# A hybrid encoder layer on one core: the seven-product sums accumulated in PSUM, and w_out's operands split in their own stage

## The chip, the cores and the metric

The kernel runs on one core of one Trainium2 chip. The metric is the device time of one launch in microseconds (us), the median of the runs shown. A core has TensorE (PE, matmuls into PSUM), VectorE (DVE), ScalarE (ACT), GpSimd (POOL) and SyncE (SP, whose queue issues the DMAs here). PSUM has eight banks of 128 x 512 float32; a matmul writes one of them.

## The reference

One layer on x of 1024 tokens by 1024 features, all float32:

```
h = rmsnorm(x); q, k, v, r, decay, u, g_a, g_b = split(h @ w_in)
o = gated linear attention, 4 heads, forward and backward scans in chunks
y_a = (rmsnorm(o) * gain * silu(r)) @ w_branch
y_b = (centred means of u over 2/4/8/16 tokens, minus u, @ w_pool) * scale
x = x + (sigmoid(g_a) * y_a + sigmoid(g_b) * y_b) @ w_out
gate, up = split(rmsnorm(x) @ w_ffn_in)          # 2 x 2816 columns
x = x + (silu(gate) * up) @ w_ffn_out
return rmsnorm(x)
```

## The kernel before

Every float32 operand is split into two float32r parts, hi (a cast on ACT, L181) and lo (a subtraction, L182, on DVE or POOL), and each product is three matmuls, hi x hi, hi x lo, lo x hi (`products`, L252). Five large projections go further: each 2 x 2 block product is done with seven block products in place of eight (Winograd's form of Strassen's scheme). Call them P1 to P7; the four results are P1+P2, P1+P6+P5+P3, P1+P6+P7+P4 and P1+P6+P7+P5, so that partial sums such as P1+P6 are shared. Before, each of the seven products is accumulated in a PSUM bank of its own and evicted into partial sums in SBUF by ACT (a copy of P1) and DVE (adds).

The stages, with their start in the profiled execution: attention (about 80 to 345 us, overlapped with the projection of r), gate units (419), branch projection (633), merged projection through w_out (720), FFN in (804), FFN out (1236 to 1456).

- **Attention.** Each head's products wait for decay scans on DVE, exponentials on ACT and the split of keys (`kt`). Beside it run jobs from a generator, `beside` (L556): one job per tick, ticks counted by matmuls in `pump`. A job may be a sum on POOL (L584), then a cast on ACT (L578), a subtraction on DVE (L569), and some ticks later a put to DRAM (L565). `branch_jobs` prepares w_branch's sums; `output_jobs` (L500) prepares all seven operands of w_out, split into hi and lo, `wo_out`.
- **Gate units** (`Gates`, L1136, ten units of seven products of 12 matmuls, 512 wide). Each unit's weights are combined on DVE (L848), cast on ACT and subtracted on POOL, four products ahead. Units 0 and 1 feed the pooling branch, whose work on DVE (L946 to L960) runs beside units 2 and on. Banks come in turn from all eight.
- **Branch and merged projections** (`project`, L1230). Seven products, each of two pieces c = 0, 1, each piece four column blocks m of six matmuls, so that a product holds four banks. Branch pieces load w_branch's operands and split them; merged pieces (`merged_piece`, L1061) load hi and lo of `wo_out`. `collect_branch` evicts into u2 and v2 and merges with the gates; `merge` adds on DVE, multiplies on DVE, adds on POOL. `collect_out` (L1430) adds to x in SBUF, some of it on POOL.
- **FFN in** (`Gated`, L1483): 22 units of seven products. Partial sums p16 and p167 on DVE; `put_out` (L1534) makes four sums of each pair of units for the last projection and writes them to DRAM.
- **FFN out** (L1735 on): seven products of 11 steps of 128 rows, four banks each, results added to x in SBUF by `collect` (L1719), some on POOL. The g operand's lo part is made on POOL, the weight's on DVE.

The orders of the products are written out by hand: GATES, BRANCH, MERGED, ORDER and OUT_ORDER. Engines run their instructions in program order. PSUM banks come from two pools, ps_mm (3) and ps_g (5), and a tile's bank is free again after its last use.

## Time and profile before

| | us |
|---|---|
| median of 3 runs | 1461.8 (1461.52 to 1464.29) |
| profiled execution | 1464.93 |
| its span | 1463.1 |
| PE busy in it | 1391.6 |
| mean granted clock | 0.988 |

The profile comes from one execution. A row of a timeline gives start and length in us, engine, line, operation, the tile written and those read, and in brackets the idle time before it and who ended it. A row of a window gives busy time and count by engine, then the clock granted to PE (1.00 is full), the DMA share and GB/s. A group row ends with busy us, mean ns of one, and idle time before with its releasers. Matmuls overlap, so that their lengths (0.39 us) exceed the distance of their starts (0.22 us).

### The profile page before, as it was taken

The page shows a single profiled execution, that of the slowest core. Times are in us where ns is not written, and L with a number is a line of the kernel's source. Part 1 is how long each engine was busy: PE and PEld are TensorE (multiplying, and loading weights), DVE is VectorE, ACT ScalarE, POOL GpSimd, SP SyncE. Part 2 cuts the span into 40 slices and gives each one's busy share as a digit, 9 for nine tenths or more (in the row PEclk, how much of TensorE's full clock was granted, in tenths as well). Part 3 has the DMA queues.
Part 4 walks back from the last instruction along what each step waited for, and adds up shares of the span by engine and source line. Part 5 has one row for each costly group of instructions (what it writes and reads, how often), then busy time and mean ns, then how long its engine had stood idle before and what let it go on. Part 6 is the DMA issues. An engine that isn't in the chain of part 4 may idle for free. (4 is left out here: it accounts for less than half of the span.)

```text
span 1463.1 us, 18944 instructions
## 1 busy us (share of the span) xinstructions
PE 1391.6 (95%) x6677; PEld 1162.3 (79%) x6677; DVE 983.9 (67%) x1263; ACT 594.3 (41%) x1057; POOL 784.0 (54%) x552
## 2 busy tenths in 40 slices
PE   7999997979999899998999989999999999999998
PEld 6888796968888678777778768888888888778876
DVE  6176868686838855667985777777777777464375
ACT  6264665653323344443225532233233224443243
POOL 3272715232243356666644457666666678597345
PEclk9999999999999999999999999999999999999999
DMA  5233445461233365796567455454444446867352
GB/s 184 73 116 112 148 169 177 159 213 62 95 93 119 116 207 188 269 385 222 205 189 255 162 180 180 158 166 158 150 153 153 157 152 230 340 238 255 130 228 89
DMA packets 174464, 257.27 MB, mean 176 GB/s; under 512 B 11384, under 2 KB 98464, under 8 KB 174368
## 3 DMA queue, kind: packets, MB, share of 16 engines
q1 hardware_dynamic: 174368, 256.05, 51.6%
q8 instruction: 53, 0.87, 0.2%
q14 instruction: 43, 0.35, 0.1%
HBM read 169.76 MB, written 86.25 MB: 175 GB/s over the span
## 5 line engine op out<-in xcount | busy, mean ns | idle before, releaser
L182 POOL TENSOR_TENSOR wl<-fs,wh 128x512 fp32r<-128x512 f32 x120 | 164.4, 1372 | 178.9 <-ACT wh L181 140.0
L254 PE MATMUL ps<-gh,wl 128*128 128x512 f32 x616 | 240.6, 391 | 3.9 <-POOL wl L182 3.8
L254 PE MATMUL ps<-gh,wh 128*128 128x512 f32 x616 | 241.2, 392 | 0.5 <-DMA wh<-u_out 0.5
L254 PE MATMUL ps<-gl,wh 128*128 128x512 f32 x616 | 240.5, 390 | 0.8 <-POOL gl L182 0.8
L181 ACT CAST wh<-fs 128x512 fp32r<-128x512 f32 x120 | 74.2, 621 | 306.4 <-DVE fs L848 294.3
L182 POOL TENSOR_TENSOR wl<-fraw,wh 128x512 fp32r<-128x512 f32 x90 | 135.5, 1505 | 49.2 <-ACT wh L181 49.1
L254 PE MATMUL ps<-hh,wh 128*128 128x512 f32 x376 | 152.3, 405 | 1.8 <-DVE ga L1156 1.2
L254 PE MATMUL ps<-hh,wl 128*128 128x512 f32 x376 | 148.6, 395 | 1.0 <-POOL wl L182 1.0
L254 PE MATMUL ps<-hl,wh 128*128 128x512 f32 x376 | 148.4, 395 | 0.0
L182 POOL TENSOR_TENSOR wl<-raw,wh 128x512 fp32r<-128x512 f32 x47 | 68.8, 1476 | 148.5 <-ACT wh L181 140.0
L254 PEld LDWEIGHTS ps<-gh,wl 128*128 128x128 f32 x616 | 116.1, 188 | 29.0 <-POOL wl L182 4.7
L254 PEld LDWEIGHTS ps<-gl,wh 128*128 128x128 f32 x616 | 116.1, 189 | 25.1 <-POOL gl L182 1.3
L254 PEld LDWEIGHTS ps<-gh,wh 128*128 128x128 f32 x616 | 116.0, 188 | 24.6 <-issue 0.9
L182 POOL TENSOR_TENSOR ol<-gor,oh 128x1024 fp32r<-128x1024 f32 (+1 forms) x42 | 108.6, 2601 | 48.5 <-ACT oh L181 46.1
L254 PE MATMUL ps<-oh,ol 128*128 128x512 f32 x308 | 120.9, 392 | 4.3 <-POOL ol L182 4.3
L254 PE MATMUL ps<-ol,oh 128*128 128x512 f32 x308 | 120.5, 391 | 2.9 <-DVE ol L182 2.9
L254 PE MATMUL ps<-oh,oh 128*128 128x512 f32 x308 | 120.6, 392 | 0.0
L182 DVE TENSOR_TENSOR ol<-wor,oh 128x1024 fp32r<-128x1024 f32 (+1 forms) x42 | 82.3, 1984 | 43.5 <-ACT oh L181 34.5
L254 PEld LDWEIGHTS ps<-hh,wh 128*128 128x128 f32 x376 | 71.8, 191 | 17.4 <-issue 2.4
L254 PEld LDWEIGHTS ps<-hh,wl 128*128 128x128 f32 x376 | 71.7, 191 | 17.4 <-POOL wl L182 1.8
L254 PEld LDWEIGHTS ps<-hl,wh 128*128 128x128 f32 x376 | 71.8, 191 | 13.4
L254 PE MATMUL ps<-wh,hh 128*128 128x256 f32 x256 | 79.5, 310 | 0.0
(274 smaller groups left out, 3315.8 us busy)
## 6 DMA issues: line engine op xcount, KB each, us to landing
fraw<-in_w_ffn_in_dram SPq DMA_DIRECT2D x44, 512.0 KB, 5.4
gor<-g_out SPq DMA_DIRECT2D x35, 512.0 KB, 6.5
wo_out<-up SPq DMA_DIRECT2D x28, 512.0 KB, 4.7
raw<-in_w_in_dram SPq DMA_DIRECT2D x48, 256.0 KB, 3.8
g_out<-s SPq DMA_DIRECT2D x44, 256.0 KB, 2.4
fraw<-in_w_in_dram SPq DMA_DIRECT2D x20, 512.0 KB, 6.2
wor<-t_out SPq DMA_DIRECT2D x20, 512.0 KB, 8.0
g_out<-g SPq DMA_DIRECT2D x33, 256.0 KB, 3.3
```

What stands on the lines that cost most here:

```text
L181: nc.scalar.copy(hi, src)
L182: eng.tensor_tensor(lo, src, as_f32(hi), op=ALU.subtract)
L254: nc.tensor.matmul(ps, a[i], b[j], start=first and n == 0, stop=last and n == 2)
```

## The change

- A product may go on in a bank that already holds a partial sum. P1, then P6, P7 and P4 share one bank (U) in units, branch and output; P2 has a bank of its own, then P5 and P3 share one (X). Where a partial sum is needed later it is copied out on ACT, or added on DVE with what stands in SBUF, and the next product then accumulates on top of it in PSUM. The orders change so that one other product stands between two of a bank where possible.
- In gate units and FFN units the adds on DVE fall from 7 to 3 and from 9 operations to 5; copies on ACT come in.
- In the merged projection P1, P6 and P7 accumulate on U, and P2 and P3 start anew on U's banks, P4 and P5 on X's; every product is added by DVE, straight from PSUM, to the blocks of x in which it counts. Three pairs follow each other on the same banks directly, one of them across the stages: P4 of branch and P1, P6 and P7, P2 and P3. POOL adds none.
- In the output projection the chains are U and X as in the units, and every bank is added to one block of x by DVE; POOL's adds to x go. P3 follows P5, and P4 follows P7, directly on the same banks.
- `output_jobs` makes only the four sums on POOL and puts them unsplit (`t_wo`, 16 puts of 256 KB). The merged pieces load them, or w_out itself, and split them as the branch pieces do.

The diff, cut to its core:

```diff
-    def products(ps, a, b, first=True, last=True):
+    def products(ps, a, b, first=True, last=True, onto=False):
         for n, (i, j) in enumerate(((0, 0), (0, 1), (1, 0))):
-            nc.tensor.matmul(ps, a[i], b[j], start=first and n == 0, stop=last and n == 2)
-    def mm3(ps, a, b, first, last):
-        products(ps, a, b, first, last)
+            nc.tensor.matmul(ps, a[i], b[j], start=first and n == 0, stop=last and n == 2, skip_group_check=onto)
+    def mm3(ps, a, b, first, last, onto=False):
+        products(ps, a, b, first, last, onto)
         pump(ps.shape[-1] / HALF)
...
+    UP = (1, 6, 7, 4)
+    FIRST = (1, 2, 5)
...
     def output_jobs(k):
         (b11, b12, b21, b22), loads = rows_of(w_out, k)
         yield from loads
-        for op, p, src in (
-            (None, 1, b11), (None, 3, b22), (None, 2, b21), (partial(psub, b11, b12, b11), 5, b11),
-            (partial(psub, b12, b22, b12), 7, b12), (partial(psub, b22, b22, b11), 6, b22),
-            (partial(psub, b21, b21, b22), 4, b21),
-        ):
-            yield op, src, wo_out[p][:, :, k, :].rearrange("n p c -> p n c")
+        for dst, a, b, p in ((b11, b12, b11, 5), (b12, b22, b12, 7), (b22, b22, b11, 6), (b21, b21, b22, 4)):
+            yield partial(psub, dst, a, b), None, t_wo[p][:, k, :]
...
     def product(unit, p, ps, right):
         for k in range(4):
-            mm3(ps[:, :], unit(p, k), tuple(t[:, k % 2, :] for t in right[p][k // 2]), k == 0, k == 3)
+            mm3(
+                ps[:, :], unit(p, k), tuple(t[:, k % 2, :] for t in right[p][k // 2]),
+                k == 0 and p in FIRST, k == 3, p not in FIRST,
+            )
...
-    GATES = (1, 6, 2, 7, 5, 4, 3)
+    GATES = (1, 2, 6, 5, 7, 3, 4)
...
-    BRANCH = (1, 2, 6, 5, 3, 7, 4)
+    BRANCH = (1, 2, 6, 5, 7, 3, 4)
...
-    MERGED = (1, 7, 6, 5, 4, 2, 3)
+    MERGED = (1, 4, 6, 7, 5, 2, 3)
+    WEIGHT_B = {1: (0, 0), 2: (1, 0), 3: (1, 1)}
...
     def merged_piece(p, c):
         def load():
...
-        def weights():
-            parts = []
-            for k in range(2 * c, 2 * c + 2):
-                hi = wts.tile([P, HALF], F32R, tag="wh", name=name("wh"))
-                lo = wts.tile([P, HALF], F32R, tag="wl", name=name("wl"))
-                for n, t in enumerate((hi, lo)):
-                    nc.sync.dma_start(as_f32(t[:, :]), wo_out[p][n][:, k, :])
-                parts.append((hi[:, :], lo[:, :]))
-            return parts
+            if p in WEIGHT_B:
+                i, j = WEIGHT_B[p]
+                return weight_load(chunk(w_out, i, j, c))
+            return weight_load(t_wo[p][:, 2 * c : 2 * c + 2, :])
         def sums():
             def block(i, j):
                 return merged[i, j][c][:, :, :]
-            if p == 7:
+            if p == 6:
                 s3s.append(slot(s="s3"))
                 sub(s3s[c][:, :, :], block(0, 0), block(1, 0))
-            elif p == 6:
...
         def make(raw):
             a = s3s[c] if p == 7 else merged[{1: (0, 0), 6: (0, 0), 5: (1, 0), 4: (1, 1), 2: (0, 1), 3: (0, 1)}[p]][c]
-            w = weights()
-            return data_split(a), w
+            return data_split(a), weight_split(raw)
         return load, sums, make
...
         def run(self, p):
-            ps = bank(next(mm_banks))
+            if p == 1:
+                self.u = bank(ps_mm)
+            elif p in FIRST:
+                self.x = bank(ps_g)
+            ps = self.u if p in UP else self.x
             product(self.unit, p, ps, right)
             ps = ps[:, :]
             x0, x1, y0, y1 = (t[:, half, :] for t in self.rows for half in range(2))
-            done = None
-            if p == 1:
-                nc.scalar.copy(x0, ps)
-            elif p == 6:
-                add(x1, ps, x0)
-            elif p == 2:
-                add(x0, ps, x0)
-                done = x0
-            elif p == 7:
-                add(y0, ps, x1)
-            elif p == 5:
-                add(y1, ps, y0)
-                add(x1, ps, x1)
-                done = y1
+            part = {1: x0, 6: x1, 5: y1}.get(p)
+            done = {2: x0, 3: x1, 4: y0, 7: y1}.get(p)
+            if part is not None:
+                nc.scalar.copy(part, ps)
+            elif p != 4:
+                add(done, ps, done)
+                ps = done
+            if done is not None and self.n >= 2:
+                nc.scalar.activation(done, ps, AF.Sigmoid)
             elif p == 4:
-                add(y0, ps, y0)
-                done = y0
-            else:
-                add(x1, ps, x1)
-                done = x1
-            if done is not None and self.n >= 2:
-                nc.scalar.activation(done, done, AF.Sigmoid)
-            if p in (4, 5) and self.n >= 2:
-                half = int(p == 5)
+                nc.scalar.copy(done, ps)
+            if p in (4, 7) and self.n >= 2:
+                half = int(p == 7)
...
-    def project(base, products, collect, before, amid=None):
+    U_BANKS = [ps_mm] * 3 + [ps_g]
+    X_BANKS = [ps_g] * 4
+    def project(base, products, collect, before, amid=None, first=FIRST, up=UP, pools_of=lambda p: U_BANKS if p == 1 else X_BANKS):
+        banks = {}
         for at, p in enumerate(products):
             before(p)
-            sums = [bank(next(mm_banks)) for _ in range(4)]
+            if p in first:
+                banks[p in up] = [bank(pool) for pool in pools_of(p)]
...
-                            c == 0 and k == 0, c == 1 and k == 1,
+                            c == 0 and k == 0 and p in first, c == 1 and k == 1, p not in first,
                         )
...
         sa, yb = (quarter(t, m) for t in gates[i, j])
-        add(dst, ps, s)
-        nc.vector.tensor_tensor(dst, dst, sa, op=ALU.mult)
+        if s is not None:
+            add(dst, ps, s)
+            ps = dst
+        nc.vector.tensor_tensor(dst, ps, sa, op=ALU.mult)
         padd(dst, dst, yb)
     def collect_branch(p, m, ps):
         u, v = quarter(u2, m), quarter(v2, m)
-        if p == 1:
-            nc.scalar.copy(u, ps)
-        elif p == 2:
-            merge(0, 0, m, ps, u)
-        elif p == 6:
-            add(u, ps, u)
-        elif p == 5:
-            add(v, ps, u)
-        elif p == 3:
-            merge(0, 1, m, ps, v)
-        elif p == 7:
-            merge(1, 1, m, ps, v)
-            add(u, ps, u)
+        if p in (1, 6, 5):
+            nc.scalar.copy(v if p == 5 else u, ps)
         else:
-            merge(1, 0, m, ps, u)
+            i, j = {2: (0, 0), 7: (1, 1), 3: (0, 1), 4: (1, 0)}[p]
+            merge(i, j, m, ps, {2: u, 7: v, 3: u}.get(p))
     x2 = [None] * NT
...
     def collect_out(p, m, ps):
-        p1, w = quarter(p1s, m), quarter(u3, m)
-        def x_of(i, j):
-            return x2[4 * (1 - i) + m][:, COLS[j]]
-        if p == 1:
-            nc.scalar.copy(p1, ps)
-            add(x_of(0, 0), x_of(0, 0), p1)
-        elif p == 7:
-            add(w, ps, p1)
-        elif p == 6:
-            add(w, ps, w)
-            add(p1, ps, p1)
-            padd(x_of(1, 1), x_of(1, 1), w)
-        elif p == 5:
-            for i in (1, 0):
-                add(x_of(i, 1), ps, x_of(i, 1))
-            add(x_of(1, 0), x_of(1, 0), w)
-            padd(x_of(0, 1), x_of(0, 1), p1)
-        else:
-            i, j = {4: (1, 0), 2: (0, 0), 3: (0, 1)}[p]
-            add(x_of(i, j), ps, x_of(i, j))
+        for i, j in {1: ((0, 0),), 6: ((0, 1),), 7: ((1, 0), (1, 1)), 5: ((0, 1), (1, 1)), 4: ((1, 0),), 2: ((0, 0),), 3: ((0, 1),)}[p]:
...
+            xs = x2[4 * (1 - i) + m][:, COLS[j]]
+            add(xs, ps, xs)
+        if p in (5, 2, 3):
             t = 4 * (1 - i) + m
             if p != 3:
                 mss[t] = vec(2, "n2ms")
                 xn[t] = slot(shape=(D,), s="xn")
...
-    project(len(BRANCH) * 2, MERGED, collect_out, before_out, amid_out)
+    project(
+        len(BRANCH) * 2, MERGED, collect_out, before_out, amid_out, (1, 2, 3, 4, 5), (1, 2, 3, 6, 7),
+        lambda p: X_BANKS if p in (4, 5) else U_BANKS
+    )
...
-            self.banks[p] = bank(next(mm_banks))
-            product(self.unit, p, self.banks[p], split_b)
-            ps = self.banks[p][:, :]
+            if p == 1:
+                self.u = bank(ps_mm)
+            elif p in FIRST:
+                self.x = bank(ps_g)
+            ps = self.u if p in UP else self.x
+            product(self.unit, p, ps, split_b)
+            self.done.add(p)
+            ps = ps[:, :]
             mul = partial(nc.vector.tensor_tensor, op=ALU.mult)
-            if p > 2:
-                p16, p167 = self.p16, self.p167
             if p == 1:
-                self.p1 = self.g[:, 0, :] if self.g else t2(s="p1")[:, :]
-                nc.scalar.copy(self.p1, ps)
+                self.sg = self.g[:, 0, :] if self.g else t2(s="sg")[:, :]
+                nc.scalar.copy(self.sg, ps)
             elif p == 2:
-                self.sg = self.p1 if 6 in self.banks else self.g[:, 1, :]
-                add(self.sg, ps, self.p1)
+                add(self.sg, ps, self.sg)
                 nc.scalar.activation(self.sg, self.sg, AF.Silu)
             elif p == 6:
-                add(p16, ps, self.p1)
+                nc.scalar.copy(self.gate, ps)
+            elif p == 5:
+                nc.scalar.copy(self.up, ps)
             elif p == 7:
-                add(p167, ps, p16)
-            elif p == 4:
+                add(self.up, ps, self.up)
+            elif p == 3:
+                add(self.gate, ps, self.gate)
+                nc.scalar.activation(self.gate, self.gate, AF.Silu)
+            else:
                 self.g = self.g or slot(s="g")
-                add(self.g[:, 0, :], ps, p167)
-                mul(self.g[:, 0, :], self.g[:, 0, :], self.sg)
-            elif p == 3:
-                add(p16, ps, p16)
-                nc.scalar.activation(p16, p16, AF.Silu)
-                mul(self.g[:, 1, :], p16, p167)
-            if p in (4, 5) and {4, 5} <= self.banks.keys():
-                self.fifth()
-        def fifth(self):
-            for s in (self.p167, self.p16):
-                nc.vector.tensor_tensor(s, self.banks[5][:, :], s, op=ALU.add)
+                mul(self.g[:, 0, :], ps, self.sg)
+            if p in (3, 7) and {3, 7} <= self.done:
+                self.g = self.g or slot(s="g")
+                mul(self.g[:, 1, :], self.gate, self.up)
...
-    OUT_ORDER = (1, 6, 2, 5, 3, 7, 4)
+    OUT_ORDER = (1, 2, 6, 5, 3, 7, 4)
...
     def collect(p, m, ps):
-        p1 = p1s[m // 2][:, m % 2, :]
-        if p == 1:
-            nc.scalar.copy(p1, ps)
-            plus(nc.gpsimd, 0, 0, m, p1)
-        elif p == 6:
-            nc.vector.tensor_tensor(p1, ps, p1, op=ALU.add)
-            plus(nc.vector, 0, 1, m, p1)
-            for j in (1, 0):
-                plus(nc.gpsimd, 1, j, m, p1)
-        else:
-            for half, j in {2: ((0, 0),), 5: ((0, 1), (1, 1)), 3: ((0, 1),), 7: ((1, 1), (1, 0)), 4: ((1, 0),)}[p]:
-                plus(nc.vector, half, j, m, ps)
+        half, j = {1: (0, 0), 2: (0, 0), 6: (0, 1), 5: (1, 1), 7: (1, 1), 3: (0, 1), 4: (1, 0)}[p]
+        xs = x2[4 * half + m][:, COLS[j]]
+        add(xs, ps, xs)
         if p == 3:
...
+    banks = {}
     for at, p in enumerate(OUT_ORDER):
         closing = at == len(OUT_ORDER) - 1
-        sums = [bank(next(mm_banks)) for _ in range(4)]
+        if p in FIRST:
+            banks[p in UP] = [bank(pool) for pool in (U_BANKS if p == 1 else X_BANKS)]
+        sums = banks[p in UP]
...
-                piece_product(sums[m], n, m, i == 0, i == n_of - 1)
+                piece_product(sums[m], n, m, i == 0 and p in FIRST, i == n_of - 1, p not in FIRST)
...
-                    piece_product(sums[m], at * n_of + i, m, False, i == n_of - 1)
+                    piece_product(sums[m], at * n_of + i, m, False, i == n_of - 1, p not in FIRST)
```

More of the change, by code (lines that the diff above doesn't have):

```diff
@@ L464 @@
     s_out = {p: dram.tile([P, 4, HALF], F32, name=f"s_out{p}") for p in (3, 5, 6, 7)}
-    wo_out = {p: dram.tile([2, P, 4, HALF], F32, name=f"wo_out{p}") for p in range(1, 8)}
+    t_wo = {p: dram.tile([P, 4, HALF], F32, name=f"t_wo{p}") for p in (4, 5, 6, 7)}
     READY = 2
@@ L1416, in two_scale @@
         return rs
-    p1s, u3 = ([slot(s="sum") for _ in range(2)] for _ in range(2))
     mss = {}
@@ L1671 @@
     x2 = []
-    p1s = [slot(s="p1s") for _ in range(2)]
     gain_final = slot(shape=(D,), s="gfin")
```

29 lines of the change are left out of this document (13 added, 16 removed).

## The prediction

> **What bounds the kernel now.** I read the page's engine rows, then the chain that ended last, then a table of 20 us windows, then the waits of PE, and at each place where PE lost time the timelines around it.
>
> ```profile
> span 1463.1 us, 18944 instructions
> ...
> PE 1391.6 (95%) x6677; PEld 1162.3 (79%) x6677; DVE 983.9 (67%) x1263; ACT 594.3 (41%) x1057; POOL 784.0 (54%) x552
> ```
>
> ```profile
> PE 35%; DVE 4%; POOL 2%; issue 2%; ACT 2%; DMA 1%; SPq 0%; POOLq 0%; ACTq 0%; DVEq 0%
> ```
>
> PE is the bound: it idles 1463.1 - 1391.6 = 71.5 us of the span, and no other engine has more than a few per cent of the chain. The change keeps every matmul (three per 128-row step, seven products), so it can only change those 71.5 us, and the time that matmuls run at a lowered clock. Below, columns are window, length, then busy us and count for PE, PEld, DVE, ACT, POOL, then the granted clock.
>
> ```profile
> 220.00:240.00 20.00, 13.25 (x51) 10.24 (x50) 18.79 (x28) 9.61 (x21) 13.22 (x8) 0.83 0.77 262
> 300.00:320.00 20.00, 13.64 (x66) 11.17 (x67) 17.34 (x30) 12.46 (x24) 8.72 (x6) 0.91 0.64 193
> 480.00:500.00 20.00, 17.26 (x67) 13.47 (x68) 15.70 (x22) 7.23 (x13) 6.92 (x7) 0.91 0.49 157
> 660.00:680.00 20.00, 15.71 (x56) 12.07 (x55) 15.05 (x16) 7.00 (x10) 14.61 (x10) 0.83 0.69 253
> ...
> 1000.00:1020.00 20.00, 20.00 (x90) 16.57 (x89) 15.63 (x19) 5.70 (x10) 11.49 (x9) 1.00 0.26 87
> 1300.00:1320.00 20.00, 17.96 (x76) 14.45 (x75) 15.20 (x9) 7.44 (x9) 20.00 (x11) 0.95 0.51 180
> ```
>
> The FFN window (1000) has no hole: 90 matmuls in 20 us, 0.222 us each, 2.7 us for a product of 12. The holes lie in the attention (220, 300), a gate unit (480), the branch projection (660) and the output projection (1300). So the adds that leave DVE in the FFN (22 units of 4, at 0.68 us of a row below, 60 us) buy nothing there, and I cost the change hole by hole.
>
> **Attention: -11 us.** Today the split of w_out runs beside heads 0 to 3: 28 casts (ACT L578), 28 subtractions (DVE L569) and 28 puts of 512 KB. All go; 16 subtractions on POOL stay, with 16 puts of 256 KB. Rows: the tile written with its 28 puts, then DVE, ACT and PE around two holes.
>
> ```profile
> L565 SPq DMA_DIRECT2D wo_out<-up x28: 359/366/620, 174.7 to 310.8; - x28
> ```
>
> ```profile
> 233.21 1.28 DVE L569 TENSOR_TENSOR up<-wsum,up 128x512 fp32r<-128x512 f32 x2
> 234.41 0.68 DVE L182 TENSOR_TENSOR kt<-kp,kt 128x512 fp32r<-128x512 f32 x1
> ```
>
> ```profile
> 229.48 0.62 ACT L578 CAST up<-wsum 128x512 fp32r<-128x512 f32 x1 [2.84 <-POOL wsum L584]
> ```
>
> ```profile
> 233.96 0.58 PE L254 MATMUL kv<-vh,kt 128*128 128x256 f32 x1 [4.95 <-ACT kt L181]
> ```
>
> ```profile
> 309.47 1.28 DVE L569 TENSOR_TENSOR up<-wsum,up 128x512 fp32r<-128x512 f32 x2
> ```
>
> ```profile
> 309.81 0.39 PE L254 MATMUL kv<-vh,kt 128*128 128x256 f32 x1 [3.74 <-ACT kt L181]
> ```
>
> Ahead of the first hole DVE (18.79 of 20 us busy) spends 1.28 us on L569 right before the operation that ends kt, and a cast on ACT waits 2.84 us for POOL with the attention's own work behind it. Taken out of the chain that ends in kt, these two pull it 1.28 + 2.84 = 4.1 us forward; the hole of 4.95 us shrinks to about 1, and the lowered clock (0.83 in that window) goes with it, some 2.5 us, estimated from a dozen matmuls that start 0.42 us apart, as at 674.31 below, not 0.22. I put head 2 at -6.5. The jobs now take 28 ticks (four times 3 + 4), not 40 (four times 3 + 7), so they end near 175 + (311 - 175) x 28/40 = 270 us, and head 3's hole is free of them: 1.28 us of L569 stands just before kt at 309.47, and its cast on ACT too: -3.5. Heads 0 and 1: -1. Bounds: -4, if the decay scans bound these chains anyway; -17, if the two windows (20 - 13.25 and 20 - 13.64, together 13.1 us without PE) fill up and heads 0 and 1 gain the same third as much. I take the value in the middle, because DVE is the fullest engine in both windows.
>
> The Trainium skill's page "TensorE: Matmul & The Clock Gate", section "What's actually happening", says that about 3.4 us without work halve the clock and about as long a busy stretch brings it back. The trace agrees at 4.95 us (clock 0.83). It speaks against the change too: a new wait over that length would be paid twice.
>
> **Gate units: +2 us.** Per unit DVE loses 4 of 7 adds, ACT gains two or three copies of about 0.6 us (as the casts below). Each accumulating product now waits for the copy or add of the partial sum, and has one product (2.7 us) for it; today eight banks let DVE fall behind. Rows: one such add by its group, then PE, DVE and ACT:
>
> ```profile
> L1165 DVE TENSOR_TENSOR ga<-ps,ga 128x512 f32<-128x512 f32 x10 | 6.8, 684 | 2.1 <-PE ps L254 2.1
> ```
>
> ```profile
> 481.98 0.79 PE L254 MATMUL ps<-trh,wh 128*128 128x512 f32 x1 [2.79 <-DVE ga L1178]
> ```
>
> ```profile
> 491.63 4.14 DVE L952 TENSOR_TENSOR ws<-ws 128x525 f32<-128x525 f32 x3
> ```
>
> ```profile
> 497.99 0.62 ACT L181 CAST wh<-fs 128x512 fp32r<-128x512 f32 x1 [5.64 <-DVE fs L848]
> ```
>
> The wait of 2.79 us for a bank (481.98) goes, with the clock of 0.91: -3 to -5. But where pooling's chain holds DVE (4.14 us) and a cast waits 5.64 us behind it, a copy behind that cast is late by 5.64 + 0.6 + 0.6 - 2.7 = 4 us. Such stretches come with four pooling groups; I take one or two that bite, +6 against -4. Bounds -5 and +12 (three that bite).
>
> **Branch and merged projections: +5 us.** Branch: 16 DVE adds become 8 ACT copies, no loss. The hole at 670 stays, since the merges of product 2 keep their place before the splits:
>
> ```profile
> 673.71 0.80 PE L254 MATMUL ps<-dh,wl 128*128 128x512 f32 x1 [2.83 <-POOL wl L182]
> 674.31 0.63 PE L254 MATMUL ps<-dh,wh 128*128 128x512 f32 x1
> 674.73 0.63 PE L254 MATMUL ps<-dl,wh 128*128 128x512 f32 x1
> ```
>
> Merged: w_out is split in its stage: 28 casts on ACT and 28 subtractions on POOL, priced by the branch stage's own, and 14 loads of 512 KB on SP's queue in place of 56 of 256 KB.
>
> ```profile
> L182 POOL TENSOR_TENSOR wl<-wraw,wh 128x512 fp32r<-128x512 f32 x28 | 45.6, 1658 | 21.0 <-ACT wh L181 18.1 <-PE ps L254 2.9
> ...
> L181 ACT CAST wh<-wraw 128x512 fp32r<-128x512 f32 x28 | 16.5, 618 | 32.7 <-POOL wl L182 10.9 <-PE ps L254 6.3 <-issue 6.2
> ...
> L1079 POOL TENSOR_TENSOR mg<-mg,mg 128x1024 f32<-128x1024 f32 x2 | 6.7, 3377 | 0.0
> ```
>
> 45.6 us on POOL, less 8 adds that go, in a stage of 84 us: it fits, but in order. Before product 6 POOL also makes two sums of 3.4 us (L1079), with wl behind them: +2. Banks: merged product 1 follows branch product 4 on the same banks, 7 follows 6 and 3 follows 2; between the end of a bank and its next use lie 18 matmuls, 4.0 us, against 0.7 to 2 us of DVE work behind splits: +1 each. Bounds: 0, and +14 if wl is late twice as at 673.71 (2.83 us and a clock of 0.83 behind it).
>
> **FFN: +2 us.** Per unit DVE loses 4 of 9 operations (0.68 us, as above), ACT gains two copies, in a stage without holes. In mid-unit a copy has 2.7 us, and the cast ahead of it waits for a sum that DVE starts right after the last eviction: no wait. Where a pair of units ends, DVE makes four sums (L1538 to L1541), then the sum for a cast, and the copy of product 1 stands behind that cast on ACT. Today:
>
> ```profile
> 1010.26 1.66 DVE L1538 TENSOR_TENSOR s<-g,g 128x512 f32<-128x512 f32 x1
> 1011.95 0.69 DVE L1539 TENSOR_TENSOR s<-s,g 128x512 f32<-128x512 f32 x1
> 1012.56 1.78 DVE L1540 TENSOR_TENSOR s<-g 128x512 f32<-128x512 f32 x1
> 1014.26 1.78 DVE L1541 TENSOR_TENSOR s<-g,s 128x512 f32<-128x512 f32 x1
> ```
>
> ```profile
> 1017.32 0.62 ACT L181 CAST wh<-fs 128x512 fp32r<-128x512 f32 x1 [5.36 <-DVE fs L848]
> ```
>
> With the new order: from the end T of product 4, the product's multiply to T+0.9, four sums at 0.65 to 0.69 from start to start (the row without a neighbour on POOL) to T+3.5, the cast's sum to T+4.1, cast to T+4.7, copy to T+5.3; product 6 wants its bank at T+5.4. No slack: I take 0.2 us at each of 10 places. Bounds -1, +6.
>
> The Trainium skill's page "SBUF — State Buffer", section "Who interferes with whom", says that a DVE operation with two SBUF inputs shares a port pair with GpSimd's reads, and whoever came first holds the other up for a whole instruction. The trace agrees (1.66 to 1.78 us for some of these sums, 0.69 for one). Hence the price of a sum here hangs on what POOL does beside it, and the contended one is a rival below.
>
> **Output projection: -5 us.** DVE loses one add of eight per column block, POOL loses 12 adds.
>
> ```profile
> 1307.57 7.46 POOL L1687 TENSOR_TENSOR x<-x,p1s 128x512 f32<-128x512 f32 x4
> ```
>
> ```profile
> 1260.65 0.50 PE L254 MATMUL ps<-oh,ol 128*128 128x512 f32 x1 [1.70 <-POOL ol L182]
> ...
> 1317.38 0.50 PE L254 MATMUL ps<-oh,ol 128*128 128x512 f32 x1 [2.04 <-POOL ol L182]
> ```
>
> The four adds of 7.46 us hold up ol at 1317.38: 2.04 us and about 1 of lowered clock (0.95) go. The hole at 1260.65 has DMA behind it; with the gate's last operation shorter than today I take -1 of its 1.7, and -1 for smaller ones. Bounds -7 and -1: the new adjacent pairs (5 then 3, 7 then 4) wait for DVE at a distance of some 2 us.
>
> **Sum.** -11 + 2 + 5 + 2 - 5 = -7 us on the profiled execution: span 1456.1. That execution took 1464.93, 3.1 above the median of 1461.8, so I predict 1455 beside the median. All low ends together give 1432, all high ends 1489; they will not fall together.
>
> **Rivals.** (a) Slower: the sums where a pair of units ends run at their contended 1.7 us, as today. Four sums then take 5.9 us, the copy of product 1 lands at T+8.0 or so, and product 6 waits about 2.5 us at 10 places: +25, thus 1455 + 23 = 1478; more if the clock drops behind each. It decides as soon as sums, cast and copy pass two products (5.4 us). For: three of the four sums are contended today. Against: POOL is held back by the same cast then, and DVE ends its older work sooner. (b) The gate units' new waits bite at all pooling groups and wl is late in the merged stage: +12 and +10 in place of +2 and +5: 1470; with (c) together 1477. (c) The attention's holes stay, bound by the decay scans on DVE: -4 in place of -11: 1462, no change. (d) The change does more: holes of both heads closed, the branch hole at 670 too, as DVE and ACT get ahead: 1443. Against: nothing before 670 moves.
>
> **Chances.** Forecast (1448 to 1458) 0.44; (d) 0.11; (c) 0.15; (b) 0.15; (a) 0.15. The range 1441 to 1478 leaves out the far halves of (a) and (d) and a little of (b). What a measurement can tell from no change is about 0.2%, 2.9 us: faster 0.55 (forecast and d), same 0.15 (c), slower 0.30 (a and b). The likeliest case alone: 1448 to 1458.
>
> **What would show it.** Right: the waits for kt in windows 220 and 300 under 2 us and the clock back near 1.00; no wait for ol at 1317; branch hole still there; FFN windows with PE at 20.0 of 20. Wrong: PE waits on ps named after ACT copies or DVE adds of the same bank, 2 to 4 us each, at the ends of unit pairs (a) or beside pooling's L952 (b); windows 220 and 300 unchanged (c).

## The result and the profile after

The changed kernel took 1466.51 us (median of 20 runs, 1464.29 to 1472.45) against 1464.24 for the kernel before (20 runs beside them, 1461.52 to 1467.68): a ratio of 1.0018, 95% interval 1.0008 to 1.0027. It is slower by about as much as can be told from no change. The forecast was 1455, and it stood on 1461.8, the median of the first three runs of the kernel before.

The profiled execution agrees: a span of 1464.0 after 1463.1. First the page's rows of the kernel after.

```profile
span 1464.0 us, 18532 instructions
...
PE 1389.6 (95%) x6677; PEld 1159.7 (79%) x6677; DVE 810.2 (55%) x1079; ACT 628.8 (43%) x1123; POOL 769.9 (53%) x560
```

DVE has lost 174 us of work, and PE idles as long as before (74.4 us after 71.5). So the question is where the time that was won went. The table cuts both traces at the first matmul of each stage, in us, one execution each; "FFN start" is the first 28 FFN products (four units' worth). A wait of PE just ahead of a stage's first matmul counts to the stage before.

| stage | before | after | difference | forecast |
|---|---|---|---|---|
| up to the gate units (attention) | 420.5 | 410.1 | -10.4 | -11 |
| gate units | 212.1 | 212.9 | +0.8 | +2 |
| branch projection | 87.7 | 86.7 | -1.0 | together +5 |
| merged projection | 83.9 | 91.0 | +7.1 | |
| FFN start | 89.5 | 96.0 | +6.5 | together +2 |
| rest of FFN in | 342.7 | 343.0 | +0.3 | |
| FFN out | 219.8 | 217.3 | -2.5 | -5 |

The gain in the attention is there, nearly as large as forecast. It is given back in the merged projection and at the start of the FFN. The windows of the kernel after that answer to those shown of before (columns as there):

```profile
220.00:240.00 20.00, 17.44 (x85) 13.78 (x84) 16.84 (x25) 10.27 (x24) 17.64 (x12) 1.00 0.58 185
300.00:320.00 20.00, 17.32 (x91) 14.23 (x90) 13.87 (x25) 10.19 (x19) 5.10 (x4) 0.91 0.32 106
480.00:500.00 20.00, 17.07 (x67) 13.27 (x66) 14.50 (x18) 7.16 (x13) 8.10 (x6) 0.91 0.44 157
650.00:670.00 20.00, 16.33 (x59) 12.45 (x58) 14.91 (x11) 8.67 (x14) 18.12 (x12) 0.83 0.62 222
660.00:680.00 20.00, 19.15 (x74) 15.29 (x73) 8.92 (x5) 9.27 (x14) 14.24 (x10) 0.84 0.46 147
1000.00:1020.00 20.00, 20.00 (x90) 16.52 (x89) 8.45 (x13) 7.31 (x14) 10.23 (x9) 1.00 0.30 98
1300.00:1320.00 20.00, 20.00 (x90) 16.57 (x89) 14.04 (x10) 9.82 (x11) 13.54 (x6) 1.00 0.54 186
```

At 220 the clock is back at 1.00 and PE does 85 matmuls and transposes, not 51. At 300 it does 91, not 66; no wait for kt over 0.22 us is left in that window, and its clock of 0.91 goes with a wait of 2.02 us for another result of DVE (o), of which the kernel before has one too, 1.97 us long, at 327. At 1300 there is no hole. At 480 as much is lost as before. The stages from the gate units on start some 10 us earlier, so the branch's hole, in 660 to 680 before, now lies in 650 to 670: it is still there. The FFN window is full in both kernels, though DVE fell there from 15.63 to 8.45 us.

PE's waits for the keys' casts (kt), before and after, bear out the attention (us in total, times, the longest):

```profile
PE kv L254 <- ACT kt L181: 9.1, 3, 5.0
```

```profile
PE kv L255 <- ACT kt L181: 4.1, 4, 1.6
```

Next the three largest waits of PE in the kernel after. Two of them did not exist before: PE waits for a copy on ACT out of the bank that it wants to go on with.

```profile
PE ps L255 <- ACT ga L1150: 10.0, 5, 2.9
PE ps L255 <- POOL wl L182: 8.5, 11, 2.8
PE ps L255 <- ACT sums L1488: 7.5, 1, 7.5
```

**The 7.5 us at the FFN's start.** PE, then ACT, in timelines of the kernel after; the first two units run interleaved, in the order 1, 2, 5, 6, 7, 4, 3:

```profile
843.69 0.80 PE L255 MATMUL ps<-gh,wh 128*128 128x512 f32 x1 [7.52 <-ACT sums L1488]
```

```profile
834.79 1.05 ACT L181 CAST gh<-hb 128x1024 fp32r<-128x1024 f32 x1 [1.73 <-DVE hb L1385]
839.24 1.04 ACT L181 CAST gh<-hb 128x1024 fp32r<-128x1024 f32 x1 [3.40 <-DVE hb L1385]
840.19 0.58 ACT L1490 COPY sums<-ps 128x512 f32<-128x512 f32 x1
840.67 1.99 ACT L181 CAST gh<-hb 128x1024 fp32r<-128x1024 f32 x2
842.56 0.58 ACT L1490 COPY sums<-ps 128x512 f32<-128x512 f32 x1
843.04 1.08 ACT L1488 COPY sums<-ps 128x512 f32<-128x512 f32 x2
```

In these first units ACT also splits the features (gh), and those casts wait for DVE's sums (hb). The copy of product 6 (L1488) stands behind them and starts at 843.04, 10.0 us behind the start of that product's last matmul (833.06); product 7 of the first unit, on the same bank, starts at 843.69. In the kernel before the same eviction was as late, but product 7 had a bank of its own, so nobody waited. It can be read in the trace of before, where the adds of product 6 (L1516) start at 843.55:

```profile
843.55 1.28 DVE L1516 TENSOR_TENSOR sums<-ps,g 128x512 f32<-128x512 f32 x2
```

This wait is not all of the +6.5 us. The first five FFN products, ahead of it, take 21.7 us after 18.8: transposes among them wait for DVE (2.20 us at 810.7). The six from there to product 7 of the first unit take 8.3 more, the wait and the lowered clock behind it. The rest takes 4.7 less, mostly because the kernel before waits there for POOL, at 873:

```profile
873.38 0.50 PE L254 MATMUL ps<-gh,wl 128*128 128x512 f32 x1 [3.75 <-POOL wl L182]
```

**The merged stage.** POOL in the kernel after, where the branch's last sums (L1274) meet w_out's first splits (wl), PE at the start of the merged stage, and the window:

```profile
693.05 7.46 POOL L182 TENSOR_TENSOR wl<-wraw,wh 128x512 fp32r<-128x512 f32 x4
700.48 7.37 POOL L1274 TENSOR_TENSOR mg<-mg,gate 128x512 f32<-128x512 f32 x4
707.80 8.03 POOL L182 TENSOR_TENSOR wl<-wraw,wh 128x512 fp32r<-128x512 f32 x4
715.79 6.02 POOL L1274 TENSOR_TENSOR mg<-mg,gate 128x512 f32<-128x512 f32 x4
721.77 5.01 POOL L182 TENSOR_TENSOR wl<-wraw,wh 128x512 fp32r<-128x512 f32 x4
```

```profile
709.68 0.47 PE L255 MATMUL ps<-wh,dh 128*128 128x512 f32 x1 [3.01 <-DVE mg L1273]
```

```profile
700.00:720.00 20.00, 16.99 (x66) 12.90 (x65) 16.84 (x14) 5.63 (x8) 20.00 (x12) 0.91 0.29 104
```

POOL works without a pause from 693 to 727 (20.00 of 20 us in the window, the last of these rows), at 1.9 to 2.0 us for each of the first eight subtractions and 1.25 for the last four. A stage mean of 45.6 us in 84 did not show that. The wait of 3.01 us is for a bank: branch product 4's first merge on DVE starts only at 708.85, behind two subtractions (dl, 4.52 us). It lies ahead of the merged stage's first matmul, so the table has it under the branch. Of the +7.1, product 6 alone has 4.7 (16.75 us after 12.09), with these two waits for its weights, when POOL is no longer full; product 2 has 2.2:

```profile
742.08 0.50 PE L255 MATMUL ps<-wh,dh 128*128 128x512 f32 x1 [1.55 <-ACT wh L181]
743.95 0.50 PE L255 MATMUL ps<-wl,dh 128*128 128x512 f32 x1 [1.37 <-POOL wl L182]
```

**The ends of unit pairs.** Here the forecast was close. DVE's last sum, and ACT's copy of product 1, in the kernel after; product 4 ends and the next unit begins at 1011.1:

```profile
1013.79 0.68 DVE L1510 TENSOR_TENSOR s<-g,s 128x512 f32<-128x512 f32 x1
```

```profile
1015.72 0.58 ACT L1483 COPY sg<-ps 128x512 f32<-128x512 f32 x1
```

The copy ends 5.2 us behind the end of product 4 (forecast 5.3), and no wait follows. POOL is idle beside the four sums, and they take 0.69 us each; over all eleven pairs the last two of them take 0.68 us in the mean, where they took 1.58 before.

### The profile page after: what moved, and what is told of

Its sections match the earlier page's. It is cut to its first block, busy times and chain, and to the rows that moved or that the text cites. A ratio compares the mean times of both kernels' runs of the same rounds, so it can differ in the third digit from the quotient of the medians.

```text
span 1464.0 us, 18532 instructions
## 1 busy us (share of the span) xinstructions
PE 1389.6 (95%) x6677; PEld 1159.7 (79%) x6677; DVE 810.2 (55%) x1079; ACT 628.8 (43%) x1123; POOL 769.9 (53%) x560
## 5 line engine op out<-in xcount | busy, mean ns | idle before, releaser
L182 POOL TENSOR_TENSOR wl<-fs,wh 128x512 fp32r<-128x512 f32 x120 | 160.2, 1349 | 180.1 <-ACT wh L181 176.1
L182 POOL TENSOR_TENSOR wl<-fraw,wh 128x512 fp32r<-128x512 f32 x90 | 118.5, 1318 | 72.4 <-ACT wh L181 71.3
L182 POOL TENSOR_TENSOR ol<-gor,oh 128x1024 fp32r<-128x1024 f32 (+1 forms) x42 | 102.9, 2461 | 73.3 <-ACT oh L181 70.8
L182 POOL TENSOR_TENSOR wl<-wraw,wh 128x512 fp32r<-128x512 f32 x56 | 93.4, 1696 | 32.2 <-ACT wh L181 23.7
L182 DVE TENSOR_TENSOR ol<-wor,oh 128x1024 fp32r<-128x1024 f32 (+1 forms) x42 | 72.6, 1749 | 51.4 <-ACT oh L181 47.9
L1492 DVE TENSOR_TENSOR up<-ps,up 128x512 f32<-128x512 f32 x20 | 13.8, 691 | 137.1 <-PE ps L255 137.1
```

The lines of the kernel that those rows point to most:

```text
L182: eng.tensor_tensor(lo, src, as_f32(hi), op=ALU.subtract)
L1492: add(self.up, ps, self.up)
```

## The experiments

The theory at the start: an accumulating product makes PE wait for whatever stands ahead of the copy in ACT's (or DVE's) queue. The rival: splitting w_out in its own stage makes POOL and ACT late, and that is what PE feels there and at the FFN's start. Times are medians; each ratio is to the kernel before on the same chip (medians of before 1463.9 to 1465.7), with its 95% interval; stage times are cut as above, from one profiled execution each, which for e2, e9 and e17 lies 4 to 6 us from its median.

**e1_split_only.** The kernel before with the new `output_jobs` and merged weights, and no accumulation:

```diff
+        for dst, a, b, p in ((b11, b12, b11, 5), (b12, b22, b12, 7), (b22, b22, b11, 6), (b21, b21, b22, 4)):
+            yield partial(psub, dst, a, b), None, t_wo[p][:, k, :]
...
-            w = weights()
-            return data_split(a), w
+            return data_split(a), weight_split(raw)
```

> The kernel before with only the second part of the change: w_out's sums alone beside the attention, its operands split in the merged stage; no accumulation in PSUM. Theory (the loss comes from accumulating products waiting behind copies in ACT's queue): the attention gains its 10 us, the merged stage loses 3 to 6 for its splits, the start of the FFN is as before: 1457 to 1461, 4 to 7 below before. Rival (splitting in the merged stage makes POOL and ACT late, and this lateness is what PE waits for at the start of the FFN): merged stage and FFN start lose 10 to 14 here too: 1464 to 1468.

1472.03, ratio 1.0052 (1.0033 to 1.0070). Attention 408.0 (-12.5), merged stage 104.4 (+20.5), FFN start 89.4 as before. The time lies above both ranges. The rival falls, since the FFN's start is untouched; but the theory's price for the merged stage, 3 to 6 us, was wrong by 14 or more. One window of e1 where POOL is never idle and the clock falls:

```profile
710.00:730.00 20.00, 17.19 (x60) 12.80 (x61) 17.71 (x13) 6.13 (x10) 20.00 (x11) 0.83 0.34 112
```

**e2_accum_only.** The changed kernel with the old `output_jobs` and `wo_out`: the reverse of that diff.

> The changed kernel with w_out's operands split beside the attention as before, and loaded split in the merged stage; all sums still accumulate in PSUM. Theory: the holes of the attention come back (+10), the merged stage gains 3 to 5, the wait of 7.5 us for the copy of product 6 in the FFN's first units stays: 1470 to 1474. Rival (splitting in the merged stage makes the FFN's start late): that wait is gone or under 2 us and the merged stage is back at 84 us, so that only the attention's 10 us are lost against about 14 gained: 1462 to 1465.

1474.63, ratio 1.0068 (1.0050 to 1.0086). Attention 423.4, merged stage 80.4, FFN start 97.1. Accumulation alone makes the merged stage 3.5 us shorter and the FFN's start 7.6 longer, and the wait of 7.5 us stays. So each part alone is slower than both. The two meet in the merged stage: splitting costs 20.5 us there without accumulation (104.4 - 83.9) and 10.6 with it (91.0 - 80.4), of which 5.9 in product 6. That accumulation takes eight adds from POOL and some from DVE is the likely reason; no run shows it alone. The wait at the merged start is there too, though e2 splits no weights in that stage, so it belongs to the accumulation (DVE begins the branch's last four merges at 721.87 there):

```profile
722.65 0.47 PE L255 MATMUL ps<-wh,dh 128*128 128x512 f32 x1 [2.94 <-issue]
```

**e3_trio.** In the FFN's first two units product 7 starts a bank of its own:

```diff
+            if own and p == 7:
+                self.u = bank(ps_g)
...
             elif p == 7:
                 add(self.up, ps, self.up)
+                if own:
+                    add(self.up, self.up, self.gate)
...
+            elif own:
+                add(self.g[:, 1, :], ps, self.gate)
+                mul(self.g[:, 0, :], self.g[:, 1, :], self.sg)
```

> The changed kernel; in the FFN's first two units alone product 7 starts a fresh bank, so that it doesn't wait for the copy of product 6, and DVE adds the two sums in SBUF (two adds more per unit). Theory: the wait of 7.5 us goes with the lowered clock behind it: 7 to 10 less, 1457 to 1460. Rival (the features' own splits are late, whatever bank is used): the wait moves to the next product that needs a split operand: 0 to 3 less, 1463 to 1467.

1464.07, ratio 1.0000 (0.9987 to 1.0012), FFN start 92.7: 2 to 3 us less, what the rival said. But the reason was another. The wait of 7.5 us is gone, and further on PE waits for POOL, which waits for the load of w_ffn_out's first rows (wot) with weight splits queued behind it:

```profile
872.14 0.80 PE L255 MATMUL ps<-gh,wl 128*128 128x512 f32 x1 [4.53 <-POOL wl L182]
```

```profile
869.61 1.26 POOL L1534 TENSOR_TENSOR wot<-wot 128x512 f32<-128x512 f32 x1 [10.54 <-DMA wot<-in_w_ffn_out_dram]
```

**e12_late_sums**, **e8_trio_late_sums**, **e13_before_late_sums.** One edit begins those sums on POOL a unit later; e12 has it alone on the changed kernel, e8 with e3's edit, e13 on the kernel before.

```diff
-            if 0 < at < 6:
+            if 0 < at < 6 and n != 2:
                 next(summing, None)
```

> The changed kernel with only the sums of w_ffn_out's first rows begun one unit later; the FFN's first units still accumulate product 7 behind the copy of product 6. Theory (the wait of 7.5 us for the copy covered the load that POOL waits for, so that either edit alone gains little and both gain 10): the wait of 7.5 us stays, only the 1.4 us at 877 go: 1463.5 to 1466. Rival (the sums on POOL were the cause of both): the wait of 7.5 us shrinks as well, 1455 to 1460.

> The kernel in which product 7 of the FFN's first two units starts a fresh bank (e3_trio), and besides POOL's sums of w_ffn_out's first rows, which wait for their load with weight splits queued behind them, are begun one unit later. Theory (e3's gain was given back at 872, where PE waits 4.7 us for a weight split behind POOL's wait for that load): the wait of 4.7 us and its lowered clock go, 5 to 7 less than e3_trio, 1457 to 1460. Rival (the sums only move into a fuller stretch): under 2 us less, 1462 to 1465.

> The kernel before with only the sums of w_ffn_out's first rows begun one unit later. Theory: the wait of 3.8 us at 873 for POOL's split behind that load goes, with its lowered clock: 4 to 7 less than before, 1458 to 1461. Rival: DVE's and POOL's own work is late there as well, 0 to 2 less, 1463 to 1466.

e12: 1461.25, ratio 0.9987 (0.9973 to 1.0001), FFN start 93.8, between the two ranges; the wait for the copy is what it was:

```profile
842.51 0.80 PE L255 MATMUL ps<-gh,wh 128*128 128x512 f32 x1 [7.53 <-ACT sums L1488]
```

e8: 1454.59, ratio 0.9923 (0.9909 to 0.9936), FFN start 85.9, better than either range. Its windows there, against 16.31 (clock 0.83) and 18.63 in the changed kernel:

```profile
840.00:860.00 20.00, 19.11 (x84) 15.17 (x83) 15.75 (x18) 8.98 (x15) 11.60 (x6) 1.00 0.36 119
860.00:880.00 20.00, 20.00 (x89) 16.40 (x88) 12.58 (x14) 7.65 (x14) 14.39 (x11) 1.00 0.80 246
```

e13: 1460.28, ratio 0.9966 (0.9953 to 0.9978), FFN start 83.8. So e3's edit shortens the FFN's start by 3.3 us, e12's by 2.2, both by 10.1: two waits in a row covered each other. (By the ratios of the whole kernels the three are worth some 2.6, 4.5 and 13.9 us.) It also means that accumulation cost 10 us at the FFN's start in the kernel of e12 (93.8 against 83.8 in e13), not the 6.5 that the comparison of after and before shows, since the kernel before lost 5.7 there to the load. Of these 10, the copy's wait has about 8: e8, which differs from e12 in e3's edit alone, takes 7.9 less. The other 2.1 stay in e8, whose first five products take 21.7 us like those of the changed kernel; they take 18.6 to 18.8 in the three kernels that accumulate nothing (before, e1, e13). Why accumulation makes those transposes late, no run shows.

**e4_copy_first.** In the gate units the step that casts a later product's weights is issued behind the eviction:

```diff
-            if coming:
-                gunits[coming.pop(0)[0]].step()
-            elif at == 5:
+            if not coming and at == 5:
                 line_make()
             z.run(p)
+            if coming:
+                gunits[coming.pop(0)[0]].step()
```

> The changed kernel; in the gate units the step that prepares a later product's weights (a cast on ACT among it) is issued behind the eviction of the current product, not ahead of it. Theory: the copies of partial sums no longer stand behind casts that wait for DVE; of the 10.0 us that PE waits for L1150, 6 to 8 go: 1458 to 1461. Rival (DVE and ACT are simply too slow beside the pooling): the waits move to weights (wl) or to DVE's adds, under 3 us gained: 1463.5 to 1467.

1468.61, ratio 1.0031 (1.0020 to 1.0043), gate units 213.9. Nothing is gained, against the theory, and the time lies above both ranges: PE still waits for these copies, now at seven places.

```profile
PE ps L255 <- ACT ga L1150: 10.1, 7, 2.7
```

But the edit moves the weights' casts alone. In its trace a copy still stands behind a cast of the pooling branch (ph), which waited for DVE's pooling step:

```profile
452.37 0.62 ACT L181 CAST ph<-ws 128x512 fp32r<-128x512 f32 x1 [2.67 <-DVE ws L964]
452.89 0.58 ACT L1150 COPY ga<-ps 128x512 f32<-128x512 f32 x1
```

So taking the weights' casts from ahead of the copies does not end these waits. That the pooling's work on DVE is the cause is argued from this row; no run takes it away.

**The merged stage.** Five kernels take away one suspect each. e5 gives products 1 and 2 the X banks and 4, 5, 3 the U banks; e14 swaps the branch's two chains instead; both free the bank for which PE waits at the merged start. e6 moves the two sums L1076 from POOL to DVE; e10 has every second subtraction of the merged splits on DVE; e15 is e10 with e14.

```diff
-        lambda p: X_BANKS if p in (4, 5) else U_BANKS
+        lambda p: U_BANKS if p in (4, 5, 3) else X_BANKS
...
-                padd(block(1, 0), block(1, 0), block(1, 1))
+                add(block(1, 0), block(1, 0), block(1, 1))
...
-            split_to(hi[:, :], lo[:, :], raw[:, k, :], nc.gpsimd)
+            split_to(hi[:, :], lo[:, :], raw[:, k, :], second if k else nc.gpsimd)
...
-    project(0, BRANCH, collect_branch, before_branch)
+    project(0, BRANCH, collect_branch, before_branch, pools_of=lambda p: X_BANKS if p == 1 else U_BANKS)
```

> The changed kernel; in the merged projection products 1 and 2 take the X banks and 4, 5 and 3 the U banks, so that product 1 no longer follows branch product 4 on its banks and 3 no longer follows 2. Theory (the wait of 3.0 us at the start of the merged stage is for the bank, with a lowered clock behind it): 3 to 5 less than the changed kernel, 1461.5 to 1463.5. Rival (DVE is late there with the operands' split as well, and PE waits for dl instead): 0 to 1 less, 1465.5 to 1466.5.

> The changed kernel; the two sums of the merged stage that POOL makes ahead of its weight splits (L1076) are made by DVE. Theory (the merged stage's loss at 742 to 745 is a chain: DVE, POOL's sum, DVE, the cast of that sum on ACT, the weights' casts behind it, POOL's split): the chain is 2 to 3 us shorter, the two waits of 1.5 and 1.4 us and the lowered clock go: 3 to 6 less than the changed kernel, 1460.5 to 1463.5. Rival (POOL is simply full with 28 splits more): no less than 1465.

> The changed kernel; of the merged stage's weight splits every second subtraction (14 of 28) is made by DVE, not POOL. Theory (POOL is full from 690 to 730, where the branch's last sums and the first splits of w_out meet, and everything the merged stage loses comes from there): the merged stage is 3 to 6 us shorter, 1460.5 to 1463.5. Rival (DVE, 18.7 of 20 us busy at the boundary, becomes late in POOL's place): 0 to 2 less, 1464.5 to 1467.

> The changed kernel; the branch projection's two chains swap their banks, so that its product 4 ends on banks that the merged product 1 does not use, and nothing else moves. If the wait of 3.0 us at the merged start is for the bank alone, 3 to 5 less than the changed kernel: 1461.5 to 1463.5. If POOL's splits are as late as the bank (as in e5_merged_banks, where a wait of 3.2 us for wl came in its place): 0 to 1.5 less, 1465 to 1466.5.

> e14 with every second subtraction of the merged weight splits on DVE (e10). In e10 PE waited 6.3 us for the bank behind these subtractions on DVE, with no wait for wl. If bank and POOL are two limits that cover each other: both gone, branch and merged stage together 170 to 174 us (177.7 in the changed kernel), 1459 to 1463. If DVE is the limit of the boundary whatever the bank: the wait moves to dl, no less than 1465.

| kernel | us | ratio (interval) | branch + merged |
|---|---|---|---|
| changed | 1466.51 | 1.0018 (1.0008 to 1.0027) | 177.7 |
| e5 | 1473.30 | 1.0051 (1.0037 to 1.0065) | 184.6 |
| e6 | 1467.61 | 1.0013 (1.0001 to 1.0026) | 177.5 |
| e10 | 1467.32 | 1.0019 (1.0008 to 1.0031) | 178.0 |
| e14 | 1467.92 | 1.0021 (1.0006 to 1.0036) | 178.0 |
| e15 | 1467.24 | 1.0020 (1.0009 to 1.0032) | 178.3 |

None gains: e6, e10 and e15 come out as their rivals said within 1 us, e14 1.4 us above its rival's range, e5 7 us above. In each the wait that was removed stands again in another place. e5's first wait, and one of its own making (transposes that wait for ACT to evict an earlier one):

```profile
709.48 0.50 PE L255 MATMUL ps<-wl,dh 128*128 128x512 f32 x1 [3.19 <-POOL wl L182]
```

```profile
787.05 1.12 PE L1347 MATMUL tr<-ident,xn 128*128 128x128 f32 x4 [4.27 <-ACT hb L1350]
```

e6, where the weights are late at 726 instead of 742; e10, where they are in time and the bank is later, as DVE's subtractions stand ahead of its merges; e14, as e5:

```profile
726.38 0.50 PE L255 MATMUL ps<-wl,dh 128*128 128x512 f32 x1 [2.87 <-POOL wl L182]
```

```profile
713.06 0.76 PE L255 MATMUL ps<-wh,dh 128*128 128x512 f32 x1 [6.31 <-DVE mg L1273]
```

```profile
710.59 0.50 PE L255 MATMUL ps<-wl,dh 128*128 128x512 f32 x1 [3.17 <-POOL wl L182]
```

And e15, with bank and POOL both relieved: now DVE is full too (19.93 of 20), and PE waits for wl all the same.

```profile
700.00:720.00 20.00, 17.35 (x70) 13.86 (x69) 19.93 (x17) 5.19 (x8) 18.77 (x11) 0.91 0.40 137
```

So e15 does not decide whether bank and POOL cover each other: it relieves POOL only by filling DVE. No run relieves both without that. Inside the stage the loss moves as well: in e10 product 6 is cured (11.91 us in place of 16.75) and product 2 takes 17.44 in place of 14.82.

**e17_presplit.** e8 with the operands of the merged products 1 and 4 split beside the attention, as before the change.

```diff
+        yield None, b11, wo_out[1][:, :, k, :].rearrange("n p c -> p n c")
...
+            w = weights() if p in wo_out else weight_split(raw)
```

> e8_trio_late_sums, with the operands of the merged products 1 and 4 (8 of 28 splits) split beside the attention as before, and the other 20 in the merged stage. If the whole loss of the merged stage comes from its first splits meeting the branch's last sums on POOL and DVE, both full there: branch and merged stage together fall from 176.8 to 167 to 171 us, the attention gives back 1 to 4: 1447.5 to 1452 (e8: 1454.6). If the loss is spread over the 28 splits: branch and merged 173 to 176, 1454 to 1457.

1457.24, ratio 0.9946 (0.9926 to 0.9967); branch and merged together 175.3 in place of e8's 176.7, attention 416.6 in place of 412.6, in an execution 5.7 us above the run's median. With 8 of 28 splits back beside the attention a hole is back there (first row). A wait remains at the merged start, though product 1 has no weight split left in the stage, and one at 786 in product 2; the last row is DVE at the merged start:

```profile
234.56 0.39 PE L255 MATMUL kv<-vh,kt 128*128 128x256 f32 x1 [3.76 <-ACT kt L181]
...
718.47 0.47 PE L255 MATMUL ps<-wh,dh 128*128 128x512 f32 x1 [2.92 <-issue]
...
786.28 0.45 PE L1365 MATMUL tr<-ident,xn 128*128 128x128 f32 x1 [2.23 <-DVE xn L291]
```

```profile
717.69 2.47 DVE L1291 TENSOR_TENSOR mg<-ps,gate 128x512 f32<-128x512 f32 x4
```

The first row bears out the forecast's step for the attention. The second row is the bank's wait again, as in e2: PE goes on about when the first of DVE's four merges ends. By its numbers the run lies nearer to the case of a loss spread over the 28 splits, but its trace doesn't show that: product 6 is cured (10.88 us in place of e8's 16.57), and product 2, whose transposes wait for DVE, takes 19.60 in place of 14.82. What would set the stage's time with the bank's wait gone as well, no run shows.

**e9_all, e11_best, e16_best2.** e8 with e5 and e6; with e10; with e15.

> The three edits of e5, e6 and e8 together on the changed kernel. Theory: their gains add up, 3 to 5 and 3 to 6 on top of e8: 1448 to 1454, about 1% under the kernel before. Rival: the gains overlap, since the same engines are late: 1456 to 1460.

> e8_trio_late_sums with every second subtraction of the merged weight splits on DVE. Theory: the gain of e10 comes on top of e8, 3 to 6 less than 1454.6: 1448.5 to 1451.5. Rival: DVE late, 1453 to 1456.

> e15 with both edits of e8. If the limits of the boundary cover each other: 4 to 7 less than e8's 1454.6, 1447.5 to 1451. If DVE is the limit there: 1453 to 1456.

1461.57 (0.9968, 0.9953 to 0.9982), 1455.77 (0.9942, 0.9921 to 0.9964), 1458.74 (0.9965, 0.9951 to 0.9979). All three lie above the ranges of their theories, and none beats e8, the fastest kernel of this study, 0.8% under the kernel before (e11's interval overlaps with e8's). Some 0.3% of that it owes to an edit that the kernel before could have as well (e13), so that the change with e3's edit is worth 0.4%.

## Why the prediction failed, step by step

- **PE as the bound, holes costed one by one: held.** From 894 to 1236 us DVE worked 246.34 us before; in the same stretch after, 897 to 1240, it worked 149.40, and PE was busy throughout in both:

```profile
894.00:1236.00 342.00, 342.00 (x1511) 283.28 (x1510) 246.34 (x269) 103.95 (x180) 243.32 (x165) 1.00 0.50 165
```

```profile
897.00:1240.00 343.00, 343.00 (x1514) 283.56 (x1513) 149.40 (x198) 121.80 (x216) 216.56 (x164) 1.00 0.50 165
```

- **Attention -11: held** (-10.4; -12.5 in e1; 4 of it gone again in the profiled execution of e17).
- **Gate units +2: held in the sum** (+0.8), in part by luck. New waits for copies of 10.0 us stand where other waits and lags went.
- **Branch and merged +5: near in the sum** (+6.2), wrong in its working. "It fits, but in order" priced the splits at 2 us; e2 against the changed kernel puts them at 10.6, and e1 at 20.5 where POOL's adds stay. "+1 each" for the banks had 0.7 to 2 us of DVE work ahead of a bank's release; at the merged start it was 4.5 us of subtractions and a wait of 3.0. That the sum came out is luck: accumulation gave 3.5 back in the merged stage, which the forecast had at nothing.
- **FFN +2: the step that failed.** "In mid-unit a copy has 2.7 us, and the cast ahead of it waits for a sum that DVE starts right after the last eviction: no wait." That was worked out for a unit in the middle of the stage and taken for all. In the first two units the casts ahead are those of the features, the copy starts 10 us behind its product's last matmul, and PE waits 7.5 us. The measured +6.8 lies outside the bounds of -1 to +6; with the late load out of the way this wait alone costs about 8 (e12 against e8), and the products ahead of it 3 more, which the forecast had at nothing.
- **FFN out -5: too much.** The hole at 1317 went; the one at 1260 stayed, at 1263.51, with 1.38 us in place of 1.70, and so did the longest wait of the stage, 2.9 us for DVE's ol, in both kernels.

The sum of the misses: +0.6, -1.2, +1.2, +4.8 and +2.5, together 7.9 us on the span (1464.0 against 1456.1); the medians put the changed kernel another 1.4 us later (+2.3 against +0.9 between the two spans). The rest of the 11.5 us between 1466.5 and 1455 is the base: 1461.8 from three runs, 1464.24 from twenty.

Of the rivals, (a), the contended sums at the ends of unit pairs, did not come: the sums are no longer contended there. (c), no gain in the attention, did not come either. (b), waits for a bank behind a queue and late splits, is what happened, in part where it said: splits late in the merged stage it did name. Its wait for a bank came in the gate units beside the pooling (10.0 us), where other waits went in its place, and it struck most where ACT splits features, which no rival named.

The clock fell behind a wait of 3.01 us at 709.68 in the kernel after, the only long wait of a window whose clock is 0.91. The Trainium skill's page "TensorE: Matmul & The Clock Gate", section "What's actually happening", gives about 3.4 us without work as what lowers the clock. The trace differs from that: here a shorter wait sufficed, so the measured 3.0 us counts as a bound for what a new wait may cost. Why it suffices, no run tells.

## What to carry to other kernels

Before partial sums are moved into PSUM, measure in the trace of the old kernel how late each eviction runs behind its product, at every place where a stage begins or side work shares the queue: a lag that free banks used to hide becomes a wait of TensorE of the same length, less the distance to the next use of the bank (here a lag of 10.0 us, one product of 2.7 us between, and a wait of 7.5). For work that is moved into a stage, look at the busiest 20 us of every engine there and at the first product that needs the work's result, not at the stage's mean for one engine; relief of one engine alone gained nothing here. And when a cured wait gives little, look for the next one behind it before dropping the cure: here two edits worth 3.3 and 2.2 us at the FFN's start were worth 10.1 together.

## What was not expected of the hardware

A subtraction of 128 x 512 on POOL took 1.26 us where DVE rested (the row of wot in e3; DVE does nothing from 869.1 to 879.7 there) and 1.9 to 2.0 us around the start of the merged stage (7.46 us and 8.03 us for four), where DVE was busy 16.84 of 20 us; the forecast had 1.66 us. So the engine that took over the work was slower where its neighbour was busy; no run changes that alone. Moving half of the work to that neighbour (e10, e15) gained nothing.
